# One order for the sample attention's matmuls on TensorE

## The chip, the cores and the metric

The kernel runs on one core of a Trainium2 chip. The core has five engines that run their own instruction streams side by side: TensorE (PE in the rows; its weight loads are listed apart as PEld), VectorE (DVE), ScalarE (ACT), GpSimd (POOL) and SyncE (SP), which issues most of the DMAs. The metric is the device time of one execution in microseconds (us). Before the change it is 3478.62 us, the median of three runs from 3475.33 to 3484.93 us.

## The reference

One inference step of a two-layer decoder for a prompt of 1024 tokens and for a sample group of 8 sequences with 8 new tokens each. Layer 0 has two mixers, stick-breaking attention and an RWKV-7 recurrence; layer 1 is a gated short convolution; each is followed by a SwiGLU network. The change touches only the attention of the sample group, which reads 8192 cached keys and values for each of its 8 sequences through a page table:

```python
def sb_weights(z, mask):
    log_keep = jnp.where(mask, jax.nn.log_sigmoid(-z), 0.0)
    after = lax.cumsum(log_keep, axis=z.ndim - 1, reverse=True) - log_keep
    return jnp.where(mask, jnp.exp(jax.nn.log_sigmoid(z) + after), 0.0)

def sb_attend_sample(q, k_new, v_new, k_past, v_past, bias):
    z = jnp.concatenate([jnp.einsum('bqhd,bkhd->bhqk', q, k_past),
                         jnp.einsum('bqhd,bkhd->bhqk', q, k_new)], -1) * scale + bias
    w = sb_weights(z, mask)
    return (jnp.einsum('bhqk,bkhd->bqhd', w[..., :p], v_past)
            + jnp.einsum('bhqk,bkhd->bqhd', w[..., p:], v_new))
```

The weight of a key depends on the scores of all later keys, so the scores of a whole sequence are made before its weights are final: the scores run over the pages from the last to the first and carry a running sum.

## The kernel before

The work is emitted by Python generators in program order, and a scheduler then orders each engine's instructions by a time model, dependencies and priorities. The emission interleaves three kinds of work. The first is the wide work of the two layers: every product is made of three matmuls on split operands (lines 169 to 171, tiles `po`, `pg`, `pu`, `pc`, `pb`, `dn`), each with a 128x128 weight block and up to 512 columns. The second is the prompt's attention and the recurrence. The third is the sample attention, which is a stream of small steps laid between the others from about 557 us on.

A step of the sample attention handles one gather of 1 MB (128 partitions of 2048 numbers). A **scores** step (line 658 and the matmuls of line 666) gathers 128 partitions of keys into a tile `kr` and multiplies them with the queries, 16 matmuls in the program, which are 32 on the engine since fp32 takes two passes. Each fills only 32 of the array's 128 columns (`tile_position`), and four of them run side by side. After every fourth step the scores in PSUM (`zs`) go through ScalarE, VectorE and GpSimd (`stick`, lines 598 to 608). After 16 steps of a sequence a small matmul (`cps`) gives the carry between the groups, and ten exponentials (line 684) turn the scores into weights. A **values** step (line 715 and the matmuls of line 722) gathers values into a tile `vr` of the same five buffers (`KVB = 5`) and multiplies them with transposed weights, 8 matmuls in the program and 16 on the engine, again in four 32-column groups, into the one PSUM tile `vacc`. The transposes of the weights (line 707, tile `trw`, a full 128x128 array) are emitted just ahead of the first of the four values steps that use them; VectorE and ScalarE copy them to `wt`.

`sample_stream` emits scores step n, then from n = 19 on values step n - 19, and hands control back. Nothing but data and buffers ties the two on TensorE, so the scheduler may lay each burst, and each matmul of it, wherever its model sees room. The pace of the steps is set in `phase_c` by a share of the wide work (`CF`), first from `merge_ab` (22% of the steps), then inside the first segment of the layers (512 tokens). `begin` opens that segment: SyncE loads `xT`, weights and the attention output `d_o`, ScalarE and VectorE split it (`c_hi`, `c_lo`), and the first wide matmul is a `po`. When the sample steps are through, the rest of the prompt and of the recurrence follows between the wide work.

Of the kernel before, what the change touches and what calls it, by code (L numbers as in the profile page):

```python
# [17 lines left out]
P = 128  # L18
# [104 lines left out]
class Kern:  # L123
# [27 lines left out]
    def load_w(self, pool, w, cols, tag, bufs, rbufs=2):  # L151
# [9 lines left out]
        return (hi, lo) if n > 1 else (hi[:, 0], lo[:, 0])  # L161

# [449 lines left out]
    def sample_setup(self, sp, ps):  # L612
# [9 lines left out]
        self.vn = None  # L622
# [11 lines left out]
    def sample_scores(self, b, sp, ps, out):  # L634
# [18 lines left out]
        for pc in (3, 2, 1, 0):  # L653
            z = [ps.tile([P, 512], F32, tag="zs", name="zs") for _ in range(2)]
            for jj in (3, 2, 1, 0):
# [4 lines left out]
                    in_offset=bass.IndirectOffsetOnAxis(ap=self.kidx[:, b, j:j + 1], axis=0))  # L660
                kv = kr.rearrange("p (m t) -> p m t", t=P)
                for hg in range(2):
                    for c in range(2):
                        for h in range(4):
                            m = 8 * hg + 2 * h + c
                            nc.tensor.matmul(z[hg][h * 32:h * 32 + 32, jj * P:(jj + 1) * P],  # L666
                                             qbd[:, m].rearrange("p q g -> p (q g)"), kv[:, m],
                                             start=c == 0, stop=c == 1, tile_position=(0, h * 32))
# [18 lines left out]
    def sample_values(self, b, w, sp, vp, ps):  # L687
        nc = self.nc
        if self.vn is None:
            self.vn = vp.tile([TS, 512], F32, name="vn", bufs=1)  # L690
            nc.sync.dma_start(out=self.vn, in_=self.d_v[TP:, :])
        acc = ps.tile([P, 256], F32, tag="sacc", name="vacc")

        tr = ps.tile([P, 512], F32, tag="tr", name="trn")
        for hg in range(2):
            nc.tensor.transpose(tr[:TS, hg * P:(hg + 1) * P], w[hg][4][:, :TS], self.c("ident"))
        wn = vp.tile([P, 2, 32, 4], F32, tag="wn", name="wn", bufs=1)[:TS]
        nc.vector.tensor_copy(wn.rearrange("p a c g -> p (a c g)"), tr[:TS, :256])
        for hg in range(2):
            nc.tensor.matmul(acc[hg * 32:(hg + 1) * 32, :], wn[:, hg, :, 3], self.vn[:, hg * 256:(hg + 1) * 256],  # L700
                             start=True, stop=False, tile_position=(0, hg * 32))
        for j4 in (3, 2, 1, 0):
            wt = vp.tile([P, 4, 2, 32, 4], F32, tag="wt", name="wt", bufs=2)
            for hg in range(2):
                tr = ps.tile([P, 4, P], F32, tag="tr", name="trw")
                for s in range(4):
                    nc.tensor.transpose(tr[:, s, :], w[hg][j4][:, s::4], self.c("ident"))
                dst = wt[:, :, hg].rearrange("p s c g -> p s (c g)")
                if hg:
# [835 lines left out]
```

## Time and profile before

| what | us |
|---|---|
| median of three runs | 3478.62 |
| the profiled execution's own time | 3467.21 |
| its span | 3465.2 |
| TensorE busy | 3295.2 (95%) |
| VectorE busy | 2007.7 (58%) |
| ScalarE busy | 1529.5 (44%) |
| GpSimd busy | 1061.1 (31%) |

The profiled execution took 3467.21 us, 11.4 us less than the median of the three timed runs, and its span is 2 us shorter than its own time. TensorE is busy for 95% of the span. Busy is the union of the instructions' spans, and a matmul's record is longer than the distance to the next one, so a busy TensorE need not be one at its best pace; how far apart matmuls start is read from the timeline. Clock means the TensorE clock that was granted, as a share of the full 2.4 GHz; the lower level is 1.2 GHz.

### The profile page before, as it was taken

The numbers are of one execution on the slowest core, as the hardware profiler recorded it, in microseconds if no ns is written. First come the engines' busy times: TensorE is split into PE (matmuls) and PEld (weight loads), VectorE is DVE, ScalarE is ACT, GpSimd is POOL, SyncE is SP. The second block draws the span as 40 slices with busy tenths as digits, with TensorE's granted clock in tenths as the row PEclk, the third lists the DMA queues.
The fourth block names the chain that finished last, engine by engine and source line by source line (L and its number), as shares of the span: only waits on it lengthen the run. The fifth ranks groups of instructions, "written<-read, shape, count | busy, mean of one in ns | idle before, by whom it ended". The sixth has DMA issues, their size and how long they took to land.

```text
span 3465.2 us, 62165 instructions
## 1 busy us (share of the span) xinstructions
PE 3295.2 (95%) x25486; PEld 2753.2 (79%) x25486; DVE 2007.7 (58%) x3381; ACT 1529.5 (44%) x2892; POOL 1061.1 (31%) x1051
## 2 busy tenths in 40 slices
PE   7999898769999999999889999999999999999999
PEld 7989776546676777666667777679999999999999
DVE  5679555635554545633677767757555564565554
ACT  4445355634353444422466565535334342343432
POOL 1235455734454544521233232211111120121101
PEclk9999797879999999999989999999999999999999
DMA  4234437888788888764423323245322222322221
GB/s 144 89 102 142 98 92 253 289 313 340 311 311 345 349 324 344 299 239 128 120 76 99 104 78 109 80 145 166 97 74 83 77 80 68 99 86 74 91 81 52
DMA packets 222956, 558.72 MB, mean 161 GB/s; under 512 B 64208, under 2 KB 125648, under 8 KB 189904
## 3 DMA queue, kind: packets, MB, share of 16 engines
q1 hardware_dynamic: 185232, 286.10, 26.6%
q0 software_dynamic: 36864, 268.45, 20.1%
q8 instruction: 200, 3.28, 0.4%
q14 instruction: 84, 0.69, 0.1%
q10 hardware_dynamic: 576, 0.20, 0.0%
HBM read 516.09 MB, written 38.59 MB: 160 GB/s over the span
## 4 chain that ended last, share of the span: by engine, by line
PE 69%; DVE 8%; DMA 4%; ACT 3%; issue 3%; POOL 2%; SPq 1%; POOLq 0%; DVEq 0%; ACTq 0%
PE dn L169 6%; PE dn L171 5%; PE dn L170 5%; PE pg L169 5%; PE pg L170 5%; PE pg L171 5%; PE pu L170 4%; PE pu L171 4%; PE pu L169 4%; PE vacc L722 4%; PE zs L666 3%; PE pc L170 2%; PE pc L169 2%; PE pc L171 2%; DVE wl L149 1%
## 5 line engine op out<-in xcount | busy, mean ns | idle before, releaser
L149 DVE TENSOR_TENSOR wl<-wr,wh 128x1024 fp32r<-128x1024 f32 (+1 forms) x261 | 370.7, 1421 | 280.4 <-ACT wh L148 275.7
L149 POOL TENSOR_TENSOR dlo<-drw,dhi 128x1024 fp32r<-128x1024 f32 x104 | 255.5, 2459 | 795.5 <-ACT dhi L148 790.8
L148 ACT CAST wh<-wr 128x1024 fp32r<-128x1024 f32 (+1 forms) x261 | 283.7, 1088 | 442.5 <-PE pg L170 157.1
L169 PE MATMUL dn<-ahi,dhi 128*128 128x288 f32 (+1 forms) x1248 | 409.3, 342 | 27.5 <-DVE sil L1233 7.6
L1140 DVE TENSOR_TENSOR xT<-xT,dn 128x288 f32<-128x288 f32 (+1 forms) x576 | 299.2, 534 | 211.2 <-PE dn L171 205.9
L170 PE MATMUL dn<-alo,dhi 128*128 128x288 f32 (+1 forms) x1248 | 412.9, 333 | 2.1 <-DVE alo L149 2.0
L171 PE MATMUL dn<-ahi,dlo 128*128 128x288 f32 (+1 forms) x1248 | 412.4, 333 | 0.0
L169 PE MATMUL pg<-c_hi,wh 128*128 128x288 f32 (+1 forms) x1056 | 353.2, 335 | 1.1 <-ACT c_hi L148 1.1
L170 PE MATMUL pg<-c_lo,wh 128*128 128x288 f32 (+1 forms) x1056 | 351.8, 333 | 2.3 <-DVE c_lo L149 2.3
L171 PE MATMUL pu<-c_hi,wl 128*128 128x288 f32 (+1 forms) x1056 | 350.9, 332 | 1.9 <-DVE wl L149 1.9
L169 PE MATMUL pu<-c_hi,wh 128*128 128x288 f32 (+1 forms) x1056 | 351.5, 333 | 1.0 <-DVE sil L1233 1.0
L171 PE MATMUL pg<-c_hi,wl 128*128 128x288 f32 (+1 forms) x1056 | 351.4, 333 | 0.0
L170 PE MATMUL pu<-c_lo,wh 128*128 128x288 f32 (+1 forms) x1056 | 351.3, 333 | 0.0
L169 PEld LDWEIGHTS dn<-ahi,dhi 128*128 128x128 f32 x1248 | 233.8, 191 | 67.6 <-DVE xT L1140 14.8
L170 PEld LDWEIGHTS dn<-alo,dhi 128*128 128x128 f32 x1248 | 238.1, 191 | 21.0 <-issue 3.7
L171 PEld LDWEIGHTS dn<-ahi,dlo 128*128 128x128 f32 x1248 | 237.4, 190 | 20.8 <-issue 3.1
L170 PEld LDWEIGHTS pg<-c_lo,wh 128*128 128x128 f32 x1056 | 200.2, 190 | 22.2 <-issue 5.4
L169 PEld LDWEIGHTS pu<-c_hi,wh 128*128 128x128 f32 x1056 | 199.8, 189 | 21.7 <-issue 6.5
L169 PEld LDWEIGHTS pg<-c_hi,wh 128*128 128x128 f32 x1056 | 200.0, 189 | 21.3 <-issue 4.9
L171 PEld LDWEIGHTS pu<-c_hi,wl 128*128 128x128 f32 x1056 | 199.8, 189 | 20.0 <-issue 4.1
L170 PEld LDWEIGHTS pu<-c_lo,wh 128*128 128x128 f32 x1056 | 200.0, 189 | 19.3 <-issue 5.4
L171 PEld LDWEIGHTS pg<-c_hi,wl 128*128 128x128 f32 x1056 | 200.0, 189 | 18.6 <-issue 3.7
(330 smaller groups left out, 7493.4 us busy)
## 6 DMA issues: line engine op xcount, KB each, us to landing
wr<-in_w_gate_dram SPq DMA_DIRECT2D x88, 512.0 KB
wr<-in_w_up_dram SPq DMA_DIRECT2D x88, 512.0 KB
drw<-in_w_down_dram SPq DMA_DIRECT2D x88, 512.0 KB
wr<-in_w_in_c_dram SPq DMA_DIRECT2D x48, 512.0 KB
wr<-in_w_in_ab_dram SPq DMA_DIRECT2D x26, 512.0 KB
wr<-in_w_out_ab_dram SPq DMA_DIRECT2D x24, 512.0 KB
drw<-in_w_out_c_dram SPq DMA_DIRECT2D x16, 512.0 KB
Tk<-d_kT SPq DMA_DIRECT2D x20, 256.0 KB
```

Source lines behind the costliest of these rows:

```text
L148: nc.scalar.copy(hi, src)
L149: (eng or nc.vector).tensor_tensor(lo, src, hi.bitcast(F32), op=ALU.subtract)
L169: nc.tensor.matmul(out, sh, mh, start=k == 0, stop=False)
L170: nc.tensor.matmul(out, sh, ml, start=False, stop=False)
L171: nc.tensor.matmul(out, sl, mh, start=False, stop=k == n - 1)
L666: nc.tensor.matmul(z[hg][h * 32:h * 32 + 32, jj * P:(jj + 1) * P], qbd[:, m].rearrange("p q g -> p (q g)"), kv[:, m], start=c == 0, stop=c ...
L722: nc.tensor.matmul(acc[ct * 32:(ct + 1) * 32, :], wt[:, s, hg, :, g], vr[:, o:o + 256], start=(j4 == 3 and g == 0 and s == 1), stop=(j4 == ...
L1140: nc.vector.tensor_tensor(x, x, acc, op=ALU.add)
```

## The change

A new helper, `burst`, ties a TensorE instruction behind the last one it was given, so that all matmuls of the sample attention keep the order in which they are emitted. `sample_values` becomes one generator over all eight sequences. Both generators now stop once between a step's gather and its matmuls, and `sample_stream` emits in each step the gather of keys, the gather of values, the values' matmuls and then the scores' matmuls. The transposes of the next four steps' weights are emitted in the third of four values steps (`g == 2`), right behind its matmuls, two steps ahead of their first use. The closing product of a sequence (`sample_out`) is emitted behind the first values step of the next one. The arithmetic and the number of matmuls, gathers and copies stay the same.

```diff
+    def burst(self, ins):
+        if self.bursts:
+            self.tc.add_manual_dep(ins.ins, self.bursts[-1].ins.name,
+                                   mybir.DependencyInfo(mybir.DependencyClass.NoSync, mybir.DependencyReason.DATA),
+                                   reason="burst")
+        self.bursts = [ins]
...
                     in_offset=bass.IndirectOffsetOnAxis(ap=self.kidx[:, b, j:j + 1], axis=0))
+                yield 0
...
-                            nc.tensor.matmul(z[hg][h * 32:h * 32 + 32, jj * P:(jj + 1) * P],
+                            self.burst(nc.tensor.matmul(z[hg][h * 32:h * 32 + 32, jj * P:(jj + 1) * P],
...
+    def sample_weights(self, w, j4, vp, ps):
...
+        wt = vp.tile([P, 4, 2, 32, 4], F32, tag="wt", name="wt", bufs=2)
+        for hg in range(2):
+            tr = ps.tile([P, 4, P], F32, tag="tr", name="trw")
+            for s in range(4):
+                self.burst(nc.tensor.transpose(tr[:, s, :], w[hg][j4][:, s::4], self.c("ident")))
...
+    def sample_values(self, w, sp, vp, ps):
...
+        wn, wt = self.sample_new(w[0], vp, ps), self.sample_weights(w[0], 3, vp, ps)
...
+        for b in range(NB):
+            acc = None
+            for j4 in (3, 2, 1, 0):
+                for g in range(4):
+                    vr = sp.tile([P, 2048], F32, tag="kv", name="vr", bufs=KVB)
+                    nc.gpsimd.indirect_dma_start(
...
+                    yield 0
...
+                            self.burst(nc.tensor.matmul(
+                                acc[ct * 32:(ct + 1) * 32, :], wt[:, s, hg, :, g], vr[:, o:o + 256],
...
+                    if done is not None:
+                        done = self.sample_out(b - 1, done, ps)
+                    if g == 2 and j4:
+                        nxt = self.sample_weights(w[b], j4 - 1, vp, ps)
+                    elif g == 2 and b < NB - 1:
+                        nxt = self.sample_weights(w[b + 1], 3, vp, ps)
+                    elif g == 3:
+                        wt = nxt
+                    yield 1
...
-        ks, vs = scores(), values()
+        ks, vs = scores(), self.sample_values(w, sp, vp, ps)
+        self.bursts = []
         for step in range(16 * (NB + 1) + LAG):
+            v = step >= 16 + LAG
             next(ks, None)
-            if step >= 16 + LAG:
+            if v:
                 next(vs, None)
+                next(vs, None)
+            next(ks, None)
             yield 1
```

What the scheduler makes of it is read from the order in which the instructions stand on an engine. The line numbers of the changed kernel are 8 to 40 higher than those of the kernel before. The first place is on TensorE around the first norm of the layers (`ms`), where the wide work has to wait for other engines. Before:

```order
L171 MATMUL po<-c_hi,wl 128x512
L722 MATMUL vacc<-vr,wt 32x256 x8
L666 MATMUL zs<-kr,qbd_6272 32x128 x16
L1156 MATMUL ms<-nt,consts 128x512
L707 MATMUL trw<-consts,sz 128x128 x4
L722 MATMUL vacc<-vr,wt 32x256 x8
L707 MATMUL trw<-consts,sz 128x128 x12
L666 MATMUL zs<-kr,qbd_6272 32x128 x16
L722 MATMUL vacc<-vr,wt 32x256 x8
L169 MATMUL pg<-c_hi,wh 128x512
```

The same place in the changed kernel:

```order
L179 MATMUL po<-c_hi,wl 128x512
L746 MATMUL vacc<-vr,wt 32x256 x8
L674 MATMUL zs<-kr,qbd_6272 32x128 x16
L746 MATMUL vacc<-vr,wt 32x256 x8
L702 MATMUL trw<-consts,sz 128x128 x8
L674 MATMUL zs<-kr,qbd_6272 32x128 x16
L1196 MATMUL ms<-nt,consts 128x512
L746 MATMUL vacc<-vr,wt 32x256 x8
L674 MATMUL zs<-kr,qbd_6272 32x128 x16
L177 MATMUL pg<-c_hi,wh 128x512
L177 MATMUL pu<-c_hi,wh 128x512
L746 MATMUL vacc<-vr,wt 32x256 x8
```

Each values step is now followed by its scores step, with at most the transposes between them, and four whole steps stand here within three wide matmuls.

The second place is on TensorE in the last values steps, when the scores are through. Before, and then in the changed kernel:

```order
L169 MATMUL pc<-c_hi,wh 128x512
L722 MATMUL vacc<-vr,wt 32x256
L170 MATMUL pc<-c_lo,wh 128x512
L722 MATMUL vacc<-vr,wt 32x256
L171 MATMUL pc<-c_hi,wl 128x512
L722 MATMUL vacc<-vr,wt 32x256
L169 MATMUL pc<-c_hi,wh 128x512
```

```order
L179 MATMUL pb<-c_hi,wl 128x512
L739 MATMUL vacc<-vn,wn 32x256 x2
L746 MATMUL vacc<-vr,wt 32x256 x8
L769 MATMUL ops<-consts_310,vm 128x8 x4
L746 MATMUL vacc<-vr,wt 32x256 x16
L702 MATMUL trw<-consts,sz 128x128 x8
L746 MATMUL vacc<-vr,wt 32x256 x8
```

Single values matmuls that stood between single wide ones mostly stand together now.

The third place is on ScalarE at the start of the first segment, where `c_hi` is made from the loaded `d_o`. Before, and then in the changed kernel:

```order
L148 CAST wh<-wr 128x1024 x2
L148 CAST c_hi<-c_lo 128x512
L684 ACTIVATE nz<-nz,ncar 128x64 x2
L684 ACTIVATE sz<-sz,ncar 128x512 x8
L148 CAST c_hi<-c_lo 128x512 x7
```

```order
L707 COPY wt<-trw 128x4x128
L148 CAST wh<-wr 128x1024 x2
L148 CAST c_hi<-c_lo 128x512 x8
L606 ACTIVATE sz<-zs,bias_s 128x512 x2
L609 ACTIVATE se<-sz 128x512 x2
```

The ten exponentials of the second sequence stood between the casts; now the eight casts stand together and these exponentials come later.

## Rows read from the trace of the kernel before

**Rows 1.** The page: busy time, share of the span, instructions.
```profile
span 3465.2 us, 62165 instructions
PE 3295.2 (95%) x25486; PEld 2753.2 (79%) x25486; DVE 2007.7 (58%) x3381; ACT 1529.5 (44%) x2892; POOL 1061.1 (31%) x1051
```

**Rows 2.** Stretches: length, busy PE, PEld, DVE, ACT, POOL; clock, DMA share, GB/s.
```profile
726.00:744.00 18.00, 0.91 (x13) 0.48 (x6) 5.25 (x8) 10.67 (x19) 0.94 (x1) 0.50 0.87 343
744.00:1477.00 733.00, 709.91 (x6877) 514.76 (x6877) 387.05 (x519) 315.16 (x529) 352.48 (x305) 0.99 0.84 323
1477.00:1628.00 151.00, 150.96 (x730) 92.45 (x729) 49.15 (x63) 33.02 (x47) 33.91 (x30) 1.00 0.50 182
1628.00:3465.00 1837.00, 1786.03 (x12196) 1602.81 (x12194) 1112.45 (x1837) 817.36 (x1481) 353.00 (x270) 0.98 0.31 93
```

**Rows 3.** Waits of TensorE, 744 to 1628 us: total, times, longest.
```profile
PE po L169 <- issue: 17.1, 1, 17.1
...
PE cps L678 <- DVE tot L676: 2.8, 1, 2.8
...
PE vacc L722 <- DMA vr<-in_cache_v_dram,vidx: 1.5, 2, 0.8
```

**Rows 4.** Timeline of TensorE: start, duration, instruction; lone scores, lone values.
```profile
1000.67 0.40 PE L169 MATMUL pg<-c_hi,wh 128*128 128x512 f32 x1
...
1001.00 1.08 PE L666 MATMUL zs<-kr,qbd 128*32 128x128 f32 x32
...
1002.34 0.40 PE L171 MATMUL pg<-c_hi,wl 128*128 128x512 f32 x1
...
1002.81 0.40 PE L170 MATMUL pg<-c_lo,wh 128*128 128x512 f32 x1
...
1003.13 1.10 PE L722 MATMUL vacc<-vr,wt 128*32 128x256 f32 x16
...
1004.50 0.40 PE L169 MATMUL pg<-c_hi,wh 128*128 128x512 f32 x1
```

**Rows 5.** Timeline of TensorE: a scores and a values burst side by side.
```profile
1056.52 0.39 PE L169 MATMUL pg<-c_hi,wh 128*128 128x512 f32 x1
1056.83 1.08 PE L666 MATMUL zs<-kr,qbd 128*32 128x128 f32 x32
1057.73 1.05 PE L722 MATMUL vacc<-vr,wt 128*32 128x256 f32 x16
...
1059.05 0.40 PE L171 MATMUL pg<-c_hi,wl 128*128 128x512 f32 x1
```

**Rows 6.** Timeline of TensorE: single values matmuls between wide ones.
```profile
1528.84 0.50 PE L171 MATMUL pc<-c_hi,wl 128*128 128x512 f32 x1
1529.27 0.65 PE L722 MATMUL vacc<-vr,wt 128*32 128x256 f32 x2
1529.85 0.50 PE L169 MATMUL pc<-c_hi,wh 128*128 128x512 f32 x1
```

**Rows 7.** DMA issues: count, median us to landing (744-1477; 1117.8-1118.2; 1250.9-1254 us).
```profile
vr<-in_cache_v_dram,vidx POOLq DMA_INDIRECT x97, 8.8
kr<-in_cache_k_dram,kidx POOLq DMA_INDIRECT x93, 9.0
...
kr<-in_cache_k_dram,kidx POOLq DMA_INDIRECT x1, 5.7
...
vr<-in_cache_v_dram,vidx POOLq DMA_INDIRECT x1, 11.3
```

**Rows 8.** Timelines of GpSimd and TensorE: a values gather and its reader.
```profile
1216.35 0.94 POOL L715 DMA_INDIRECT vr<-in_cache_v_dram,vidx  x1 [3.19 <-PE zs L666]
...
1233.37 1.05 PE L722 MATMUL vacc<-vr,wt 128*32 128x256 f32 x16
```

**Rows 9.** Timeline of ScalarE ahead of the first segment.
```profile
735.42 0.62 ACT L148 CAST c_hi<-c_lo 128x512 fp32r<-128x512 f32 x1 [2.13 <-DMA c_lo<-d_o]
735.94 0.58 ACT L684 ACTIVATE nz<-nz,ncar 128x64 f32<-128x64 f32 x2
736.43 4.99 ACT L684 ACTIVATE sz<-sz,ncar 128x512 f32<-128x512 f32 x8
741.33 3.72 ACT L148 CAST c_hi<-c_lo 128x512 fp32r<-128x512 f32 x7
```

More of the change, by code (lines that the diff above doesn't have):

```diff
@@ L694, in sample_values, with sample_new @@
+    def sample_new(self, w, vp, ps):
+        nc = self.nc
         tr = ps.tile([P, 512], F32, tag="tr", name="trn")
         for hg in range(2):
[L696 removed]
+            self.burst(nc.tensor.transpose(tr[:TS, hg * P:(hg + 1) * P], w[hg][4][:, :TS], self.c("ident")))
         wn = vp.tile([P, 2, 32, 4], F32, tag="wn", name="wn", bufs=1)[:TS]
         nc.vector.tensor_copy(wn.rearrange("p a c g -> p (a c g)"), tr[:TS, :256])
[L699 to L701 removed]
@@ L702, in sample_values @@
[L702 to L709, printed above, removed]
-                    nc.vector.tensor_copy(dst, tr)
-                else:
-                    nc.scalar.copy(dst, tr)
-            for g in range(4):
-                vr = sp.tile([P, 2048], F32, tag="kv", name="vr", bufs=KVB)
-                nc.gpsimd.indirect_dma_start(
-                    out=vr, out_offset=None, in_=self.vview,
-                    in_offset=bass.IndirectOffsetOnAxis(ap=self.vidx[:, b, 4 * g + j4:4 * g + j4 + 1], axis=0))
-                for s in range(4):
-                    for hg in range(2):
-                        ct = (s % 2) * 2 + hg
-                        o = s * 512 + hg * 256
-                        nc.tensor.matmul(acc[ct * 32:(ct + 1) * 32, :], wt[:, s, hg, :, g], vr[:, o:o + 256],
-                                         start=(j4 == 3 and g == 0 and s == 1), stop=(j4 == 0 and g == 3 and s >= 2),
-                                         tile_position=(0, ct * 32))
-                yield 1
@@ L728, in sample_values, with sample_out @@
+    def sample_out(self, b, m, ps):
+        nc = self.nc
         ops = ps.tile([P, 512], F32, tag="tr", name="ops")
         for k in range(4):
-            nc.tensor.matmul(ops[:, k * 8:(k + 1) * 8], m[:, (k % 2) * P:(k % 2 + 1) * P],
-                             self.c("sel")[:, (k // 2) * 8:(k // 2) * 8 + 8], start=True, stop=True)
+            self.burst(nc.tensor.matmul(ops[:, k * 8:(k + 1) * 8], m[:, (k % 2) * P:(k % 2 + 1) * P],
+                                        self.c("sel")[:, (k // 2) * 8:(k // 2) * 8 + 8], start=True, stop=True))
```

45 lines of the change are left out of this document (32 added, 13 removed).

## The prediction

> **What bounds the kernel now.** I read the page first: TensorE is busy for 95% of the span, no other engine for more than 58% [rows 1]. The share by stretches comes second, because the change lies in one of them. From 744 to 1477 us scores and values steps run together between the wide matmuls: TensorE is busy for 710 of 733 us at a clock of 0.99, and the DMA engines for 84%. From 1477 to 1628 us only values steps are left: TensorE 151 of 151 us, DMA 50%. Behind that the wide work fills 1786 of 1837 us [rows 2]. So a microsecond that TensorE saves before 1628 us moves all that follows forward, provided that the DMA can follow. Third, the waits: between 744 and 1628 us TensorE waited 1.5 us for values in all, and 17.1 us at once for the first `po` [rows 3]. The gathers are early now. What TensorE loses in these stretches it loses as issue time at each change between wide and sample work, which the waits hardly show and the timeline does.
>
> **Term 1, the visits.** I call a run of sample instructions between two wide matmuls a visit. Wide matmuls start 0.235 us apart (1002.34 and 1002.81 are two apart). A lone scores burst takes 1002.34 - 1000.67 = 1.67 us from the wide start before it to the second one behind it, so it costs 1.67 - 0.47 = 1.20 us; a lone values burst 1004.50 - 1002.81 - 0.47 = 1.22 us [rows 4]. Both in one visit cost 1059.05 - 1056.52 - 0.47 = 2.06 us [rows 5]. Joining a pair saves 0.36 us. A single values matmul costs 1529.85 - 1528.84 - 0.23 = 0.78 us [rows 6], against an eighth of 1.22, or 0.15 us, in a whole burst: 0.63 us each.
>
> Along TensorE's order, from the first `po` to the last `ops`, I count 243 visits before and 135 now. Of the 108 that go, 39 are single values matmuls (54 to 15), 28 held only transposes (31 to 3), 41 are others that are joined. Singles: 39 x 0.63 = 24.6 us. Joined: 41 x 0.36 = 14.8 us. The transposes are the same number of passes, so I count nothing for their 28 visits; but inside a burst they stand between 32-column work on both sides, and such edges rise from 68 to 78. An edge that joining takes away is worth 0.36 us or less, so ten cost at most 3.6; I take 3 us. Term 1: -36 us. Bounds: -25 if only the singles count; -49 if each of the other 69 visits gives 0.36.
>
> **Term 2, the start of the first segment.** TensorE stood from 726 to 744 us with 0.9 us of work [rows 2]. The wide work needs the casts to `c_hi`; one of eight ran at 735.4, then 0.6 + 5.0 us of exponentials stood before the other seven [rows 9]. In the new order the eight stand together: up to 5.6 us. The steps that stand ahead of the first `po` are also one values and two scores steps fewer, so with five buffers up to three gathers of 1.05 MB leave the stretch in which the DMA was busy for 87% at 343 GB/s [rows 2]: up to 9 us. No row shows how much of those 9 us reaches `c_hi`, so I take 7 us of the 14.6, a little more than the first part alone. The three steps come back later: two scores steps at 2.06 - 1.22 = 0.84, a values step at 0.86 and the new keys' scores, which I put at one more scores step: 3.4 us. Term 2: -4 us, bounds -11 and +3 (nothing gained).
>
> **Term 3, the gathers' lead.** Five buffers serve both kinds. A values gather is issued when a scores burst gives its buffer back and is read two steps later: issued at 1216.35 behind scores, read at 1233.37, a lead of 17.0 us [rows 8]. In the new order values stand ahead of scores in a joint burst, so the lead is two periods less one burst, and where the scheduler puts steps close together it shrinks: at the first norm four steps stand within three wide matmuls. Pricing the new order with the costs of term 1, I get for its 114 values gathers a median lead of 14 us (18 for the order before, near the one shown). A gather lands 8.8 us after its issue in the median, 5.7 us when it goes out alone, and 11.3 us as one of three close together [rows 7]. Two leads are under 5.7 us, short by 1.4 us in all; six under 8.9 us, short by 14; eighteen under 11.3, short by 39. A values gather is now the first of a pair, behind a pause, which speaks for less than 8.8; but all five close places lie where weights are loaded too. One late gather also delays the next burst's need, so the shortages don't simply add. I take +10 us, with the ends +1 and +39. On TensorE everything behind the waiting matmul waits, wide work too.
>
> By the Trainium skill, DMA: Bandwidth & Descriptors, section Anatomy of one DMA, a DMA issued from GpSimd takes about 2.0 us plus its bytes at 436 GB/s, an estimate of 4.4 us for this gather, so the term would be near nothing and the total some 9 us lower. The trace doesn't agree: alone it took 5.7 us, usually 8.8, and the measurement decides.
>
> **Term 4, the transposes two steps earlier.** For the first weights of a sequence they now stand 5 to 7 us of TensorE work behind `cps`. Of the ten exponentials the first four must be through: 0.58 + 2 x 0.62 = 1.8 us [rows 9], and a VectorE copy before them. If ScalarE is just then in a run of casts of 3.7 us [rows 9] the transposes come late, and the scores behind them. Seven sequences at 0 to 1.5 us: +3 us, bounds 0 and +10. The later weights of a sequence have long been ready. The copies to `wt` have two steps instead of none and cost nothing; if they were late the next values step would wait 1 us, as now.
>
> **Sum.** -36 - 4 + 10 + 3 = -27 us on the profiled execution's 3467.2 us: 3440. That execution lies 11.4 us under the median of the runs, so I forecast 3478.6 - 27 = 3451 us. With every bound at its good end the change is -59, at its bad end +27: 3419 and 3506.
>
> **Rivals.** *Every gather is in time.* The pairs go out with a pause before them and land as the lone one did. Terms 3 and 4 are then 1 and 0 us, and the sum is -39 to -45: 3436. For it: DMA at 84% and no wait before [rows 2, 3]. Against it: four steps at one place.
>
> *The DMA sets the pace.* Gathers that are issued in pairs land like the close ones, at 11.3 us. Term 3 is then +39 and the sum -36 - 4 + 39 + 3 = +2; with joined bursts landing slightly sooner I take 3476. For it: the DMA is busy for 84% of a stretch that is to become shorter with the same bytes. Against it: 84% leaves 117 us of 733, far more than the 36 to be saved.
>
> *The chain stalls at each step.* One order on TensorE means that a late gather of values holds back scores whose keys are there, and wide work behind. If 96 joint steps wait 0.7 us each, that is +67, and the sum is -36 - 4 + 67 + 3 = +30: 3509. It decides from about 0.5 us a step, where the waits eat terms 1 and 2. For it: before, scores and values could pass each other. Against it: the median lead of 14 us against 8.8. It would also pull the clock: with TensorE idle from 726 to 744 us the clock was 0.50, against 0.99 in the busy stretch behind [rows 2]. The Trainium skill, TensorE: Matmul & The Clock Gate, on HAM oscillation, tells of a kernel in which each tile's wait for a DMA brought the clock down to half again; the trace agrees for the one long wait, and no run here shows it yet for short ones.
>
> That the bursts are not joined is no rival: the order shows it.
>
> **Chances.** The forecast has 0.60, and its own range is 3436 to 3466. Gathers in time: 0.15. DMA pace: 0.14. The chain: 0.11. A measurement of this kernel can tell 0.3%, 10.4 us, from no change. Faster by more, under 3468, are the forecast nearly whole and the first rival: 0.74; the DMA's pace and the forecast's upper edge give 0.15 within it; the chain 0.11 slower. The range, 3427 to 3480, leaves out the chain and the best corner.
>
> **What would show it.** Right: visits on TensorE of about 2.1 us that hold values and then scores; values-only stretch shorter by some 20 us (it held most of the singles); the wait ahead of the first `po` under 17 us with the casts together; waits for `vr` at the first norm and few elsewhere; DMA share above 0.84. Wrong: `vr` waits spread over the whole stretch, or a clock under 0.95 between the first `po` and the end of the scores, would show the chain; a first `po` as late as before would strike term 2; transposes that wait for exponentials at seven places, by more than 1.5 us each, would show term 4 too small.

## The result, and the profile after

The changed kernel takes **3432.1 us** (median of 4 runs, 3428.7 to 3437.7) beside 3477.8 us for the kernel before in the same comparison: a ratio of 0.9867, 95% interval 0.9847 to 0.9887. In a second comparison it took 3424.6 us beside 3473.4, 0.9855 (0.9838 to 0.9872). The forecast was faster, 3451 us within 3427 to 3480; the gain is 46 to 49 us where 27 were forecast.

The page of the changed kernel's profiled execution (3432.9 us, at the median of its runs) answers to [rows 1]. TensorE does the same 25486 instructions in 31 us less busy time, and its share is still 95%:

```profile
span 3431.1 us, 62168 instructions
PE 3263.9 (95%) x25486; PEld 2760.9 (80%) x25486; DVE 1998.3 (58%) x3381; ACT 1531.7 (45%) x2892; POOL 1063.4 (31%) x1051
```

The stretches of the changed kernel, with the columns of [rows 2]: the gap ahead of the first `po`, the joint scores and values up to the second norm and on to the last scores, values alone, and what follows the last `ops`.

```profile
726.00:740.00 14.00, 0.00 (x0) 0.00 (x0) 4.96 (x6) 5.09 (x8) 0.00 (x0) 0.53 1.01 396
740.00:1421.00 681.00, 653.18 (x6379) 489.87 (x6379) 362.70 (x496) 306.48 (x518) 332.72 (x287) 0.98 0.85 325
1421.00:1488.00 67.00, 65.53 (x683) 48.36 (x687) 37.48 (x45) 26.18 (x41) 41.36 (x35) 0.93 0.84 323
1488.00:1600.00 112.00, 112.00 (x683) 75.28 (x673) 41.68 (x57) 29.67 (x43) 26.74 (x26) 1.00 0.57 221
1600.00:3431.00 1831.00, 1788.49 (x12183) 1605.59 (x12181) 1111.31 (x1837) 816.92 (x1481) 352.00 (x270) 0.98 0.31 93
```

The scores end 11 us later than before (1488 against 1477 us) and the values alone take 112 us up to the last `ops`, which end at 1600.2 us; before they took some 156, up to 1632.7. What follows takes 1831 us, as before [rows 2]. So all of this profile's gain was made before 1600 us, where it was forecast.

Where it comes from is easiest to see in the busy time of TensorE from the first `po` to the last `ops`. The kernel before, and its second profiled execution:

```profile
744.00:1633.00 889.00, 865.87 (x7631) 611.44 (x7631) 438.90 (x585) 349.76 (x577) 386.39 (x334) 0.99 0.78 297
```
```profile
740.00:1631.00 891.00, 866.65 (x7629) 610.95 (x7627) 438.72 (x584) 349.74 (x576) 385.83 (x334) 0.99 0.78 297
```

The changed kernel, and its second one:

```profile
740.00:1600.00 860.00, 830.71 (x7734) 613.51 (x7734) 441.87 (x598) 362.33 (x602) 400.83 (x347) 0.98 0.81 312
```
```profile
741.00:1595.00 854.00, 828.46 (x7737) 612.37 (x7737) 438.31 (x599) 361.56 (x603) 400.70 (x347) 0.98 0.82 314
```

Busy time falls from 866 to 830 us, by 35 to 38, although the stretch now holds about a hundred instructions more (the steps that came back behind the first `po`). Idle time is 23 and 24 us before, 29 and 26 after. The clock works against the gain: it is 0.99 before and 0.98 after. Length times the missing share of the clock, summed over the clock levels in the trace, is the clock loss below: 8.5 us in this stretch in both profiles of the kernel before, 19.0 and 14.6 us in those of the changed one.

The waits of TensorE in the changed kernel, 740 to 1600 us, answer to [rows 3]:

```profile
PE po L177 <- issue: 16.0, 1, 16.0
PE vacc L746 <- DMA vr<-in_cache_v_dram,vidx: 10.5, 5, 3.4
PE cps L686 <- DVE tot L684: 6.7, 3, 3.7
```

All five waits for values lie between 810 and 860 us, around the first norm, as the same view of that window says. A visit of the changed kernel on TensorE's timeline (start, duration, instruction), with weights' transposes inside:

```profile
1087.46 0.39 PE L179 MATMUL dn<-ahi,dlo 128*128 128x512 f32 x1
1087.78 1.10 PE L746 MATMUL vacc<-vr,wt 128*32 128x256 f32 x16
1088.82 1.23 PE L702 MATMUL trw<-consts,sz 128*128 128x128 f32 x8
1089.98 1.08 PE L674 MATMUL zs<-kr,qbd 128*32 128x128 f32 x32
1090.99 0.50 PE L177 MATMUL dn<-ahi,dhi 128*128 128x512 f32 x1
```

It takes 3.53 us from the wide start before it to the one behind it.

### The profile page after: what moved, and what is told of

Same layout as the page of the kernel before. It is cut to its first block, busy times and chain, and to the rows that moved or that the text cites. A ratio compares the mean times of both kernels' runs of the same rounds, so it can differ in the third digit from the quotient of the medians.

```text
span 3431.1 us, 62168 instructions
## 1 busy us (share of the span) xinstructions
PE 3263.9 (95%) x25486; PEld 2760.9 (80%) x25486; DVE 1998.3 (58%) x3381; ACT 1531.7 (45%) x2892; POOL 1063.4 (31%) x1051
## 4 chain that ended last, share of the span: by engine, by line
PE 68%; DVE 8%; DMA 5%; issue 3%; ACT 3%; POOL 2%; SPq 1%; POOLq 0%; DVEq 0%; ACTq 0%
PE dn L177 6%; PE dn L178 5%; PE dn L179 5%; PE pg L178 4%; PE pg L177 4%; PE pu L177 4%; PE pg L179 4%; PE pu L179 4%; PE pu L178 4%; PE vacc L746 3%; PE zs L674 3%; PE pc L178 2%; PE pc L177 2%; PE pc L179 2%; DVE wl L149 1%
## 5 line engine op out<-in xcount | busy, mean ns | idle before, releaser
L177 PEld LDWEIGHTS dn<-ahi,dhi 128*128 128x128 f32 x1248 | 234.5, 191 | 60.7 <-DVE xT L1180 11.5
L732 POOL DMA_INDIRECT vr<-in_cache_v_dram,vidx x128 | 135.8, 1061 | 259.1 <-PE vacc L746 239.5
```

The costliest lines, as they stand in the source:

```text
L177: nc.tensor.matmul(out, sh, mh, start=k == 0, stop=False)
L732: nc.gpsimd.indirect_dma_start(out=vr, out_offset=None, in_=self.vview, in_offset=bass.IndirectOffsetOnAxis(ap=self.vidx[:, b, 4 * g + j4: ...
```

## The experiments

One table first. "Visits" and "edges" are counts along TensorE's order from the first `po` to the last `ops` (the two marks): runs of sample instructions between wide matmuls, and changes between 32-column and 128-column work inside them. The times in us are the start of the first `po`, the end of the last `ops`, what lies between them, and what follows up to the end, each in the profiled execution; then the median of the timed runs and the ratio to the kernel before beside it, with its 95% interval.

| kernel | visits / edges | first po | last ops | between | behind | median | ratio |
|---|---|---|---|---|---|---|---|
| before | 243 / 68 | 743.6 | 1632.7 | 889.1 | 1832.5 | 3477.8 | 1 |
| before, again | 243 / 68 | 739.5 | 1631.2 | 891.7 | 1836.8 | 3475.9 | 0.9996 (0.9981-1.0011) |
| changed | 135 / 78 | 740.1 | 1600.2 | 860.1 | 1830.9 | 3432.1 | 0.9867 (0.9847-0.9887) |
| changed, again | 135 / 78 | 740.7 | 1594.6 | 853.9 | 1828.2 | 3424.6 | 0.9855 (0.9838-0.9872) |
| transposes ahead of values | 139 / 52 | 739.8 | 1588.7 | 848.9 | 1845.3 | 3438.8 | 0.9900 (0.9885-0.9916) |
| late transposes | 161 / 50 | 752.1 | 1610.2 | 858.1 | 1847.0 | 3456.1 | 0.9949 (0.9932-0.9966) |
| scores first | 223 / 59 | 737.7 | 1619.7 | 882.0 | 1844.9 | 3464.5 | 0.9963 (0.9947-0.9979) |
| no ties | 252 / 71 | 740.5 | 1620.8 | 880.3 | 1852.9 | 3474.1 | 0.9995 (0.9985-1.0005) |
| ties alone, on before | 205 / 48 | 744.4 | 1619.3 | 874.9 | 1837.3 | 3461.3 | 0.9963 (0.9950-0.9977) |
| four gather buffers | 130 / 76 | 740.3 | 1649.6 | 909.3 | 1844.1 | 3492.3 | 1.0043 (1.0028-1.0058) |
| small work first, lag 2 | 130 / 39 | 722.7 | 1593.0 | 870.3 | 1844.5 | 3443.7 | 0.9915 (0.9898-0.9931) |
| transposes ahead, lag 2 | 116 / 51 | 732.2 | 1604.4 | 872.2 | 1834.8 | 3436.7 | 0.9883 (0.9863-0.9903) |
| lag 2 | 121 / 67 | 733.5 | 1613.8 | 880.3 | 1842.1 | 3459.1 | 0.9952 (0.9934-0.9970) |
| six gather buffers | 148 / 53 | 753.9 | 1612.5 | 858.6 | 1827.3 | 3437.5 | 0.9894 (0.9876-0.9912) |

**The changed kernel and the kernel before, once more.** No edit.

> The changed kernel once more, beside the next three on one chip, so that they can be set against it as well as against the kernel before. Both theories: 0.987 of the kernel before, about 3432 us, 135 visits of the sample attention's matmuls in the trace. Were the 46 us between the medians partly chance between chips, the ratio would come out nearer to 0.990, which is what the two profiled executions (3467.2 and 3432.9 us) give.

It gave 0.9855, so the difference between the medians is no chance of one comparison. The 0.990 of the two profiled executions did not come.

> The kernel before once more, for a second profiled execution: the profile shown took 3467.2 us where the median of its runs is 3477 to 3479. If the 11 us between are chance in the granted clock, the second profile differs from the first in how long stretches of the same work take, with the same waits on tiles, and lies anywhere between 3467 and 3487 us; the rival is that one wait or landing was other in the first profile, which would show as one stretch that is longer by most of the difference.

Its profiled execution took 3469.9 us, and no stretch of the table differs from the first by more than 4.3 us. It was a quick one again, so neither reading of the expectation was decided: no slower execution of the kernel before was profiled. Both profiled executions of the kernel before lie at the quick end of its timed runs (3466 to 3487 us in this comparison), and those of the changed kernel do not. So the profiles show a mean difference of 39.7 us between the spans (34.1 for the first pair), the medians 46 to 49. What the other 6 to 9 us are stays open. The first `po` started at 739.5 instead of 743.6 us here: 4 us from one execution of the same kernel to the next.

**No ties.** Emission order and early transposes as changed, without the dependencies:

```
-        if self.bursts:
+        if False:
```

> The changed kernel without the one order on TensorE: the order in which the code issues the matmuls and the early transposes stay, only the ties between them go. In the program's order 252 visits instead of 135, 71 inner edges instead of 78. The four runs before give 0.37 us for a visit and 0.24 us for an inner edge between the first po and the last ops (849 to 889 us over 135 to 243 visits). Theory 'visits': 117 x 0.37 - 7 x 0.24 = +42 us in that stretch, 896 us where the changed kernel has 854 to 860; in all 3466 us, or up to 3481 where the work behind it falls as in the three variants before, 15 us worse. Rival 'the early transposes and the new order of issue carry the gain': the stretch at most 875 us, in all at most 3450.

With 252 visits the kernel takes as long as the one before. But between the first `po` and the last `ops` it takes 880 us: the theory had 896 and the rival at most 875, so neither is right in size, and the total fits the theory only because of a loss behind. TensorE's busy time in that stretch is back near the old figure (866 before, 828 to 831 changed):

```profile
741.00:1621.00 880.00, 862.21 (x7612) 611.66 (x7611) 426.17 (x582) 350.63 (x575) 393.82 (x334) 0.99 0.80 302
1621.00:3473.00 1852.00, 1803.52 (x12180) 1614.44 (x12178) 1111.20 (x1836) 815.99 (x1480) 355.55 (x270) 0.98 0.30 92
```

So the ties carry the saved busy time; the idle time, 18 us against 23 and 24 before, is lower without them, and that is most of what order and early transposes give by themselves (880 us against 889 and 892). The second row is a loss that nobody forecast: the work behind the last `ops` takes 1852 us instead of 1831. More on that below.

**Ties alone, on the kernel before.** The dependency on its scores', transposes' and values' matmuls, in the order in which that kernel issues them:

```
-                            nc.tensor.matmul(z[hg][h * 32:h * 32 + 32, jj * P:(jj + 1) * P],
+                            self.burst(nc.tensor.matmul(z[hg][h * 32:h * 32 + 32, jj * P:(jj + 1) * P],
...
-                    nc.tensor.transpose(tr[:, s, :], w[hg][j4][:, s::4], self.c("ident"))
+                    self.burst(nc.tensor.transpose(tr[:, s, :], w[hg][j4][:, s::4], self.c("ident")))
```

> The kernel before with nothing but the ties between its scores', transposes' and values' matmuls in the order in which it issues them. In the program's order 205 visits instead of 243 and 48 inner edges instead of 68. Theory 'visits' by 0.37 and 0.24 us: -14 - 5 = -19 us on the stretch from the first po to the last ops, 870 us, and about 3455 us in all (3448 to 3467). Rival 'ties alone stall TensorE at every set of weights, for the copy out of PSUM': 32 sets at about 1 us give the 19 us back and more, 3474 to 3500, with waits on wt of over 20 us in the sum.

875 us between the marks and 3461 us in all, as the theory had it (870 and 3455, within its bounds). The rival fell: the one wait on `wt` is 1.1 us. Set side by side, between the marks: before 889 and 892; order and early transposes without ties 880; ties without them 875; both 854 to 860. The parts alone save some 10 and 15 us, together 33.

**Late transposes.** The ties stay, the weights are transposed directly ahead of their first use:

```
+                    if g == 0:
+                        wt = self.sample_weights(w[b], j4, vp, ps)
...
-                    if g == 2 and j4:
-                        nxt = self.sample_weights(w[b], j4 - 1, vp, ps)
```

> The one order on TensorE stays, but the weights are transposed directly ahead of the first values that use them, as in the kernel before. Theory 'the two steps of lead are what lets the chain stand': in the program's order 161 visits (26 more, of them 9 more lone values matmuls: 9 x 0.63 + 17 x 0.36 = +12 us), 50 inner edges instead of 78 (-9), and in the 18 visits that hold transposes and the values behind them TensorE stands for the copy out of PSUM, 1.0 to 1.5 us each, +18 to +27: about 3457 us (3445 to 3470), the waits showing at the values matmuls on a copy of the weights (wt). Rival 'other matmuls fill the wait, the lead is worth nothing': 3432 to 3437 us, and under 5 us of waits on wt.

The time came out as expected (3456), the reason did not. The waits of TensorE in this kernel, 725 to 1610 us, name no `wt` among the largest:

```profile
PE cps L686 <- DVE tot L684: 18.2, 3, 14.1
PE vacc L748 <- DMA vr<-in_cache_v_dram,vidx: 8.8, 5, 4.9
```

Other matmuls fill the copies' time, as the rival said. Of the 34 us between this span and that of the changed kernel beside it, 11 are a first `po` that starts at 752.1 (one wait of 14.1 us for `tot` stands ahead of it, while the wide work waits behind the sample's in TensorE's queue), 4 lie between the marks, and 19 behind them. The 14.1 us can be followed: `tot` (VectorE, 743.99 us) stands in VectorE's order behind the split of a weight block, which waits for ScalarE's `wh` cast, and that one for the DMA of `wr`. For term 4 of the forecast this says: the two steps of lead are worth some 4 us between the marks, and not by hidden copies, since waits on `wt` are 1.7 us. What the 4 us are was not taken apart: TensorE's busy time is 829 us here and 828 there, with 26 visits more, 28 edges fewer and 133 instructions fewer in the stretch.

**Transposes ahead of the values**, so that they stand next to wide matmuls:

```
+                    if g == 2 and j4:
+                        nxt = self.sample_weights(w[b], j4 - 1, vp, ps)
...
-                    if g == 2 and j4:
-                        nxt = self.sample_weights(w[b], j4 - 1, vp, ps)
```

> The weights' transposes (128 wide) are issued ahead of a step's values matmuls instead of behind them, so that they stand next to the wide matmuls and not between two narrow groups. In the program's order this leaves 139 visits instead of 135, 6 lone values matmuls instead of 15, and 52 edges between wide and narrow matmuls inside visits instead of 78. Theory 'every edge is paid': 26 fewer inner edges at some 0.33 us each are -8.6, four more visits at 0.36 are +1.4, nine fewer single matmuls save 0.27 each, -2.4: about 3422 us, 10 under the changed kernel (bounds 3416 to 3430). Rival 'only coming from and going back to the other work costs': 3432 us, within 3 of the changed kernel. Second rival 'the transposes now hold up the values behind them, their copies and buffers being late': 3436 us or more, with waits of the transposes over 5 us in the sum where the changed kernel has 0.7.

The price of an edge is seen directly. The same three groups on TensorE in this kernel, with the transposes last because they joined the visit before:

```profile
1085.31 0.39 PE L179 MATMUL dn<-ahi,dlo 128*128 128x512 f32 x1
1085.63 1.10 PE L750 MATMUL vacc<-vr,wt 128*32 128x256 f32 x16
1086.55 1.06 PE L674 MATMUL zs<-kr,qbd 128*32 128x128 f32 x32
1087.54 1.23 PE L702 MATMUL trw<-consts,sz 128*128 128x128 f32 x8
1088.53 0.48 PE L177 MATMUL dn<-ahi,dhi 128*128 128x512 f32 x1
```

3.22 us instead of 3.53. The changed kernel's visit goes from 128 columns to 32, to 128, to 32 and back to 128; here the transposes stand next to a matmul of their own width, so that one change to the other width and back is gone, for 0.31 us. Between the marks the kernel takes 849 us, 5 less than the changed one beside it, with 14 us less of busy time (814.2 against 828.5), so the theory holds there, at about half the net size: 9 us of it came back as idle time. The forecast of the total, 3422 us, missed: the kernel is 14 us slower than the changed one, because what follows the last `ops` takes 1845 instead of 1828 us. The total lies where the second rival had it, but the rival's waits on transposes did not come (1.1 us).

**What lies behind the marks.** In that part the code is the same in all kernels, but its schedule is built on where the sample's work ends, and in TensorE's order it differs from kernel to kernel for some 510 to 680 us behind the last `ops` (350 in the one with six buffers), until the orders agree again. Of the 17 us between the variant with transposes ahead and the changed kernel's second profile, 4 are idle time of TensorE (46.9 against 42.6 us) and 12 are clock loss (38.1 against 25.9). Two short stretches of the variant show where the clock loss arises (slices of 8 us, columns as in [rows 2]):

```profile
1916.00:1924.00 8.00, 7.26 (x46) 5.36 (x44) 5.23 (x7) 6.14 (x11) 2.09 (x2) 1.00 1.02 270
1924.00:1932.00 8.00, 6.59 (x57) 4.41 (x57) 7.23 (x11) 4.81 (x10) 0.14 (x1) 0.73 0.25 63
1932.00:1940.00 8.00, 8.00 (x36) 5.98 (x36) 2.80 (x6) 4.84 (x11) 2.10 (x4) 0.50 0.19 60
1940.00:1948.00 8.00, 8.00 (x66) 5.72 (x65) 6.22 (x12) 2.15 (x5) 1.27 (x1) 0.92 0.25 74
2044.00:2052.00 8.00, 8.00 (x45) 6.17 (x45) 4.68 (x6) 6.65 (x11) 2.14 (x2) 1.00 1.04 297
2052.00:2060.00 8.00, 4.57 (x32) 3.02 (x30) 7.89 (x12) 5.93 (x10) 2.02 (x2) 0.83 0.34 96
2060.00:2068.00 8.00, 8.00 (x25) 5.88 (x26) 7.85 (x14) 5.28 (x10) 4.22 (x4) 0.50 0.44 130
2068.00:2076.00 8.00, 8.00 (x52) 6.84 (x51) 6.97 (x13) 1.32 (x3) 1.30 (x1) 0.81 0.08 18
```

TensorE misses 2.15 us of the first two slices, and its granted clock falls to 0.50, the lower of its two levels; it misses 3.4 us at 2052, and falls again. In the changed kernel (its second profile) no slice from 1900 to 2092 us misses more than 0.9 us, and only one of them shows a lower clock:

```profile
1924.00:1932.00 8.00, 7.13 (x65) 4.74 (x64) 6.46 (x9) 5.26 (x10) 3.80 (x4) 1.00 0.63 176
2060.00:2068.00 8.00, 7.71 (x35) 5.97 (x34) 7.92 (x15) 2.93 (x5) 3.40 (x3) 0.79 0.21 66
```

Over the variants, "behind" is 1827 to 1853 us with no relation to the visits. The kernel before and the changed one both have short ones. What it is made of can be read: over the fourteen profiles TensorE's idle time behind the marks runs from 43 to 57 us and the clock loss from 26 to 43, and what is left when both are taken off is 1752 to 1761 us everywhere. Which of the waits behind the marks a given change moves was not settled.

**Scores first.** Scores ahead of values in each step:

```
             next(ks, None)
             if v:
                 next(vs, None)
-                next(vs, None)
             next(ks, None)
+            if v:
+                next(vs, None)
```

> Scores stand ahead of the values in each step, everything else as changed. In the program's order the bursts fall apart: 223 visits instead of 135 (45 lone values matmuls instead of 15, 59 inner edges instead of 78), though chain and early transposes are kept. Theory 'visits are what the change saves': 30 x 0.63 + 58 x 0.36 - 19 x 0.33 = +34 us, less 5 to 9 for values gathers that are read half a step later: about 3459 us (3450 to 3468). Rival 'the gain is the order and the early transposes, not the visits': 3423 to 3432 us, since only the lead of the values' gathers changes, and it grows.

28 us more between the marks (882 against 854), where the theory had 27: visits, not ties or early transposes as such, make the difference. The rest of the 40 us between the medians lies behind the marks (1845 against 1828).

**Four buffers for gathers** instead of five:

```
-KVB = 5
+KVB = 4
```

> The changed kernel with four buffers for the gathered keys and values instead of five: 130 visits, 76 inner edges, so visits are as in the changed kernel (-2 us). What changes is the gathers' lead, by about one gather's pace, 4.7 us. Theory 'the lead of the gathers is a term of its own': the values' gathers had 3.6 to 5.0 us to spare at the median, so about half come late; waits on gathers rise from 10 us to 25 to 45 us, and the stretch from the first po to the last ops from 854 to about 875 us; in all 3445 us (3435 to 3465). Rival 'landing is quick enough at any lead, since fewer transfers are in flight': waits at most 15 us and 3420 to 3431.

The largest term of all, and under-sized by more than half: the stretch grew by 55 us where 21 were expected, and 3492 us lies outside the 3435 to 3465. The waits of TensorE in it, 740 to 1650 us, and the same stretch as a window:

```profile
PE vacc L746 <- DMA vr<-in_cache_v_dram,vidx: 36.1, 16, 6.2
PE po L177 <- issue: 16.2, 1, 16.2
PE dn L177 <- ACT ahi L148: 9.3, 3, 3.9
```
```profile
740.00:1650.00 910.00, 847.99 (x7794) 625.70 (x7795) 442.19 (x601) 362.99 (x604) 409.27 (x350) 0.96 0.80 299
```

Waits for values rise by 26 us, as expected. The rest of the 55 is some 10 us of other waits and the clock: 0.96 over 910 us against 0.98 over 854, a loss of 39.9 us against 14.6, and TensorE's busy time rises by 20 us although it makes five visits fewer. The mechanism of the forecast's rival in which the chain stalls is seen here at work, though at sixteen steps and not at each: late gathers hold up wide work, and the clock pays once more. The Trainium skill, TensorE: Matmul & The Clock Gate, on HAM oscillation, tells of waits for DMA per tile that bring the clock down again and again; this trace agrees in kind, with sixteen waits of up to 6.2 us and a clock of 0.96.

**Six buffers** (room from the scores' buffers; transposes ahead of values as above):

```
-KVB = 5
+KVB = 6
...
-                                                        st[hg], tag="s", bufs_z=10, bufs_e=2)
+                                                        st[hg], tag="s", bufs_z=8, bufs_e=2)
```

> The variant with the weights' transposes ahead of the values, and six buffers for gathered keys and values instead of five; their room comes from the scores' buffers, eight instead of ten, which the transposes two steps ahead give back sooner. In the program's order 148 visits and 53 inner edges (that variant with five buffers: 139 and 52). Theory 'the lead of the gathers is a term of its own' (one buffer fewer cost about 50 us in the stretch): waits of TensorE on values' gathers behind the first po fall from 7.8 us to under 3, the last ops stand at 1586 us (1588.7 there, -5 to -8 for waits, +3 for nine visits; bounds 1578 to 1590); behind it 1828 to 1850 us, so 3417 to 3436 in all, and if the work behind falls as in the changed kernel the quickest of all. Rival 'eight buffers for scores hold up the sticks': waits on sz, D_ or zs, and the last ops at 1595 us or later.

Waits for values behind the first `po` fell to 4.1 us from 7.8, where under 3 were expected, and the last `ops` came at 1612.5 us, where the rival had them. The waits from 725 us on, and two lines of ScalarE's timeline:

```profile
PE zn L652 <- ACT sz L606: 15.1, 2, 13.0
PE vacc L750 <- DMA vr<-in_cache_v_dram,vidx: 12.6, 4, 8.4
```
```profile
738.58 1.04 ACT L148 CAST wh<-wr 128x1024 fp32r<-128x1024 f32 x1 [27.50 <-DMA wr<-in_w_out_ab_dram]
...
743.24 0.68 ACT L606 ACTIVATE sz<-zs,bias_s 128x512 f32<-128x512 f32 x1
```

The scores of the new keys (`zn`) wait 13.0 us until ScalarE has read an earlier scores tile, and ScalarE reads it behind casts of weights that wait for their DMA, 27.5 us at the first one. The first `po` starts at 753.9 us, 14 us later than with five buffers. So the rival's time came, but a wait for one of the eight buffers is not shown. Between the marks the kernel takes 10 us more than with five buffers, with a clock of 0.97 instead of 0.99.

**A lag of two steps**, alone, with the transposes ahead of the values, and with all small work moved:

```
-LAG = 3
+LAG = 2
```

> The changed kernel with the values two steps behind the scores' end instead of three and nothing else: 121 visits, 67 inner edges. Theory 'visits and edges': 14 x 0.37 + 11 x 0.24 = 8 us off, the last ops at 1587 us; in all 3417 to 3441 us by what the work behind takes (1828 to 1853 us so far). Rival 'two steps bring waits': the last ops at 1594 us or later, in all 3424 to 3449 us.

> The variant with the weights' transposes ahead of the values, and the values two steps behind the scores' end instead of three: 116 visits and 51 inner edges in the program's order, the fewest so far. Theory 'visits and edges', 0.37 and 0.24 us: 19 x 0.37 + 27 x 0.24 = 13.5 us off, the last ops at 1581 us where the changed kernel beside it had 1594.6. What comes behind the last ops took 1828 to 1853 us in the runs so far, and is a matter of how the rest of the work falls: 3411 to 3436 us in all, under the changed kernel (0.9855 of before) only if it falls as there. Rival 'with two steps the values meet gathers and exponentials that are late', as in the other variant with two steps (the last ops at 1593 us, 9 later than the sums gave): the last ops at 1590 to 1597 us and 3420 to 3450 in all.

For the third, beside LAG = 2 and the transposes ahead as above:

```
+                    if done is not None and g == 1:
+                        done = self.sample_out(b - 1, done, ps)
...
+                        wn = self.sample_new(w[b + 1], vp, ps)
                         nxt = self.sample_weights(w[b + 1], 3, vp, ps)
```

> The changed kernel with all 128-wide matmuls of a step put ahead of its values: weights' transposes, those of the new tokens (issued with the weights' two steps ahead), and the output's matmuls one step later; and values two steps behind the scores' end instead of three. In the program's order 130 visits, none of a lone values matmul, and 39 inner edges instead of 78. Theory 'visits and edges' by 0.37 and 0.24 us: -2 - 9 = -11 us on the stretch from the first po to the last ops, 843 us where the changed kernel beside it had 854; in all 3414 us if the work behind falls as in the changed kernel, 3429 if it falls as in the variant with transposes ahead. Rival 'edges inside a visit are free': the stretch at 852 us or more. Second rival, waits: the exponentials of a sample come late for transposes one step sooner, over 10 us of waits on them.

All three missed: the last `ops` came at 1614, 1604 and 1593 us, where counts alone gave 1587, 1581 and about 1584. In the first two the rival with waits was nearer, but the total of the first lies 10 us above its bound and the last `ops` of the second 7 us behind it. In the third, the waits on exponentials stayed under 2 us. Fewer visits did not pay, since TensorE stands 45 to 48 us of the stretch instead of 26 and the clock is 0.97, a loss of 24 to 30 us where the changed kernel has 15 and 19. The largest waits in the first of them, 725 to 1614 us:

```profile
PE po L177 <- issue: 19.8, 1, 19.8
PE vacc L746 <- DMA vr<-in_cache_v_dram,vidx: 15.7, 8, 4.2
PE dn L177 <- DVE sf L616: 6.8, 3, 3.9
```

The prices of 0.37 us a visit and 0.24 us an edge, with which these runs were forecast, are a fit to four of the runs above, in which TensorE stands 23 to 35 us of the stretch, and as a forecast of the whole stretch they hold only there. No variant beats the changed kernel.

## Why the prediction was right, point by point

- **Term 1, the visits: -36 forecast.** TensorE's busy time between the marks fell by 36.7 us (mean of two profiles each), and the three steps that came back, put at 3.4 us in term 2, are paid in it; so about -40, within the bounds. The clock, for which the sum has no term, hides part of it: its loss in the stretch rose from 8.5 us to 16.8 (means of two), so at an unchanged clock the visits would stand at up to -48, an estimate, close to the bound of -49. The visits in the trace are the 243 and 135 that were counted. That they and not something else are the cause is shown by the kernel without ties (252 visits, busy time back at 862 us) and by scores first (223 visits, 854 us).
- **Term 2, the start: -7 earlier, 3.4 back.** The first `po` starts at 740.1 and 740.7 us, against 743.6 and 739.5 before: about -1, within what the kernel before does by itself. The mechanism came all the same, behind a segment that opens later. SyncE's first load of the segment, before and then in the changed kernel:

```profile
702.14 0.38 SPq L1314 DMA_DIRECT2D xT<-in_xT_dram  x1
```
```profile
707.20 0.38 SPq L1354 DMA_DIRECT2D xT<-in_xT_dram  x1
```

  In the second profiles it is issued at 701.9 and 708.9 us. From it to the first `po` pass 41.4 and 37.6 us before, 32.9 and 31.8 after: 7 us less in the mean, the size of the forecast. Some 4 of them are the casts. ScalarE in the changed kernel, which answers to [rows 9]:

```profile
735.51 0.62 ACT L148 CAST c_hi<-c_lo 128x512 fp32r<-128x512 f32 x1 [2.12 <-DMA c_lo<-d_o]
737.53 4.37 ACT L148 CAST c_hi<-c_lo 128x512 fp32r<-128x512 f32 x7 [1.40 <-DMA c_lo<-d_o]
```

  The exponentials no longer stand between the casts, though ScalarE now waits 1.4 us for `c_lo` there. From the first cast to the first `po` pass 8.2 us in both profiles before, 4.6 and 3.2 after. The other 3 us, from the load to the first cast, are within the 4 us by which the kernel before varies, so "up to three gathers leave the stretch" is neither shown nor refuted. What failed is a step that the term leaves out: it takes the opening of the segment as fixed, and the opening came 6 us later, which ate the gain. What moved it is not settled; one candidate stands under term 3.
- **Term 3, the gathers' lead: +10.** Waits for values behind the first `po` rose from 1.5 to 10.5 us (10.1 in the second profile), all but 0.3 us of them at the first norm, as forecast. The gathers did not come in later: in the first profile the five late ones were there 5.9 to 10.5 us after their issue, and in the changed kernel's second profile, 741 to 1483 us (count, median us to landing; compare [rows 7]):

```profile
vr<-in_cache_v_dram,vidx POOLq DMA_INDIRECT x99, 8.6
kr<-in_cache_k_dram,kidx POOLq DMA_INDIRECT x94, 9.7
```

  So the rival in which the DMA sets the pace falls by these landings, the one in which every gather is in time by the 10 us of waits, and the term is one of lead: with one buffer less it is 36 us of waits and 55 us of time. But idle time between the marks as a whole rose by only 3.3 us (24.1 to 27.4, means of two), since other waits shrank; this the sum had not seen. Nor had it seen that the lead counts ahead of the first `po` too, where sample steps already run. Waits of TensorE for values from 557 to 739 us, before and then in the changed kernel (2.7 and 18.1 us in the second profiles):

```profile
PE vacc L722 <- DMA vr<-in_cache_v_dram,vidx: 2.3, 2, 1.7
```
```profile
PE vacc L746 <- DMA vr<-in_cache_v_dram,vidx: 14.3, 5, 6.6
```

  In the same window waits for keys fell from 8.2 to 2.4 us. That these waits are what opens the segment later is not shown: with ties alone it opens at 706.8 us with only 3.3 us of them.
- **Term 4, transposes earlier: +3.** Transposes waited 0.7 us in one place, where the term had put its cost. `cps` waited 6.7 and 5.7 us, where [rows 3] have 2.8 and the second profile of before 2.9: 3 us more, within the bounds, but not at the transposes.
- **What follows: 0.** -1.6 us in the first pair of profiles, -5 in the mean of two. It was right, but by luck: in the ten variants the same work took 1827 to 1853 us. The forecast had taken it as fixed.
- **The sum.** By means of two profiles each: first `po` -1.2, busy and idle time between the marks -36.7 and +3.3, behind -5.1: -39.7 us, where -27 was forecast. The 13 us between them are 4 of visits, 10 of idle time that the sum added and that did not come (3 instead of 13), 5 behind, less 6 at the first `po`. So the range was met by terms that missed both ways, and the forecast's own range of 3436 to 3466 was not. The rest up to the 46 and 49 of the medians lies in the timed runs, and stays open.
- **Every gather in time as a rival** (3436 us) is nearer to the measured 3432 than the forecast is, but not by its mechanism: it had 1 us of waits for values, and 10 came.
- **The chain as a rival** (3509 us) did not come at five buffers: a clock of 0.98 and five waits. At four buffers something of its kind did, at 3492, with sixteen waits and a clock of 0.96, neither of them as far as the rival had it.
- **The signs.** Visits of values and then scores came. Values alone take 112 us instead of 156, 44 less where 20 were said, partly since the scores end 11 us later. The wait ahead of the first `po` is 16.0 and 17.0 us, which says little, as it is 11.5 in the second profile of before. The DMA share up to the second norm is 0.85, as said.

## What to carry to other kernels

Where a busy engine alternates between two kinds of work, count the changes along its order and price one from the timeline: that gave 36 us of 866 within a few us, and a change of width inside a visit costs about as much as one at its ends (0.31 us there and back, against 0.36 us for two bursts joined). An order forced on an in-order engine is only as good as the lead of what feeds it: look at how far the slowest input is ahead before tying it, since one buffer less turned a gain of 46 us into a loss of 17 (3492.3 against 3475.4 beside it). And judge a variant by the stretch that it changes as well as by its total: the work behind it, the same in all, moved by up to 25 us in idle time and clock.

## What the runs showed that was not expected

- In two places a short gap of TensorE was paid twice. At 1916 to 1932 us of the variant with transposes ahead it missed 2.15 us, and the clock stood at 0.73, 0.50 and 0.92 in three slices of 8 us, some 6.8 us of full speed lost; at 2052 it missed 3.4 us, and 0.83, 0.50 and 0.81 followed, 6.9 us.
- One wait of 14.1 us with late transposes, at a matmul of the sample that stands ahead of the first `po` in TensorE's order, moved the start of the wide work by 11 us. It hangs on a weight's DMA through ScalarE's and VectorE's order, as the 13.0 us with six buffers do through ScalarE's; why the scheduler laid them so was not tried.
- The first `po` of one and the same kernel moved by 4.1 us between two executions, as much as the net forecast of term 2.
